# Four-layer hybrid trunk: gate modulation as columns, a third raw weight buffer, an earlier first load, two-pass gate weights

## The chip, the cores and the metric

The kernel runs on 1 core of a Trainium2 chip. The metric is the device time of one execution in microseconds (us); lower is better. The engines are named as the profile does: PE (TensorE's matmuls) and PEld (its weight loads), DVE (VectorE), ACT (ScalarE), POOL (GpSimd), SP (SyncE, which here only issues DMAs). ACT issues some DMAs too.

## The reference

A diffusion trunk of four layers over a latent stream x (512 tokens) and a context stream (256 tokens), both 1024 wide in float32. Layers 0 and 3 are gated linear attention in both directions (GLA), layer 1 is windowed attention, layer 2 a bidirectional RG-LRU. Each is wrapped in normalisation and modulation from a conditioning vector:

```python
for i in range(DEPTH):                                   # 4 layers
    kind, j = i % 3, i // 3
    ctx_out = i < DEPTH - 1
    shift, scale, gate = jnp.split(s_lat @ w_mod[i] + b_mod[i], 3, axis=-1)
    shift_c, scale_c, gate_c = jnp.split(s_ctx @ w_mod[i] + b_mod[i], 3, axis=-1)
    h = rmsnorm(x, g_pre[i]) * (1.0 + scale[:, None, :]) + shift[:, None, :]
    hc = rmsnorm(xc, g_pre[i]) * (1.0 + scale_c) + shift_c
    ...                                                  # y, yc = the layer's mixer of h, hc
    x = x + gate[:, None, :] * rmsnorm(y, g_post[i])
    if ctx_out:
        xc = xc + gate_c * rmsnorm(yc, g_post[i])
# in the GLA mixer, per direction d:
la = log_sigmoid((h @ w_g1[d]) @ w_g2[d] + b_g[d]) / 16  # w_g1 is 1024 x 16, w_g2 is 16 x 512
```

## The kernel before

**Precision.** A float32 operand is held as a rounded high part and the remainder: `Rh` and `Rl` are the normalised, modulated input of both streams (transposed, 8 contraction blocks of 128), and each weight tile becomes `wh` and `wl` (`split`, L265: a cast on ACT, a subtraction on DVE, one in three on POOL). A product is three passes: high by high, high by low, low by high (`ws_part`, L380).

**Weights.** `raw()` (L218) gives 512 KB landing buffers, two in rotation, shared by the weights of the mixers (two to a weight tile, `loadw`, L223), by the modulation's weights (two to a step, `mod_part`, L507) and by some parameters. `fetch` starts one weight ahead, `convert` splits it, `weights` (L358) hands it out. All of these loads are issued in order by SP, which waits there until the buffer is free. In the first normalisation and in two finishes the modulation uses other buffers, `rawp`.

**Modulation.** `mod_part` multiplies 256 columns of `w_mod` by the two conditioning vectors (16 short PE instructions, L524). `mod_ss` (shift and scale) evicts the result, transposes it so that each channel lies on a partition, and adds bias and norm weight there in small DVE operations (L543 to L555). `mod_gate` (gate, four for each layer) loads `g_post` and `b_mod` broadcast over 128 partitions, multiplies (L573 on POOL, L574 on DVE), splits the product (L575, L576) and spreads it over all partitions by four products with a selecting matrix `sel` (L582), which DVE adds to the bias into `gpt` (L583). These steps run inside the mixers, by `background` (L596): a step is begun there and ended at the next call.

**The start.** `first_norm` (L652) loads x and the context, normalises and transposes them, and loads modulation weights in four steps of two parts; the gate weights `w_g1` are fetched ahead of step 1, the first q/k weights ahead of step 3. A hand-written order on PE, ACT and DVE then alternates the modulation products, `modulate` (L697) and the products of the gate weights (`todo[:2]`) and of q and k (`todo[2:]`) over contraction blocks (L734 to L754).

**Gates of GLA.** `load_g1` (L271) puts four copies of `w_g1` into both `wh` and `wl`; the second product (L979) then takes three groups of 32 rows, so that it has the three passes in its own contraction.

**The end of a layer.** `finish` (L758) is the output product over four weight tiles (L796), squares and gates the result (`take`, L801), adds it to the stream (`residual`, L816), normalises (`square`, L819; `scale`, L822) and transposes (`norm`) the next layer's input, two tiles of 128 tokens at a time, in a hand-written order (L884 to L933). `rstd_of` (L611) gives the inverse root in two POOL operations.

**Head 0 of GLA.** `spread` (L1259) deals the matmuls of `values` between the eight steps of `levels`; for the first head of a layer the credit is two thirds of them, and the rest follows.

Elsewhere PE's order comes from a planner that places instructions by program order, priority and its own estimate of when their inputs are ready; each engine runs its list in order.

## Time and profile before

| | us |
|---|---|
| median of three runs (1516.42 to 1520.79) | 1518.22 |
| the profiled execution | 1513.64 |
| its span | 1511.8 |
| PE busy, share of the span | 1442.0 (95%) |
| DVE busy | 1010.5 (67%) |
| ACT busy | 784.2 (52%) |
| POOL busy | 189.4 (13%) |

One execution was profiled; its span runs from the first instruction to the last, and its own time has the launch around it. A busy engine is one with an instruction running; matmuls overlap, so their spacing and not their length is what one more of them costs. "Idle before, released by" names what ended a wait. PEclk is the share of the full clock that PE was granted.

### The profile page before, as it was taken

Reading aid. Unit: us, or ns where it says so; the run is one execution under the profiler, and the core shown is the slowest. Engines: PE = TensorE matmul, PEld = TensorE weight load, DVE = VectorE, ACT = ScalarE, POOL = GpSimd, SP = SyncE. Lnnn points to the kernel's source line nnn. Section 1 sums busy time; section 2 is a strip of 40 time slices with the busy share of each in tenths; the row PEclk is TensorE's granted clock in tenths of the full one; section 3 lists DMA queues with packets and bytes.
Section 4 is the critical chain, followed back from the end, with each engine's and each line's share of the span. In section 5 each row is a group of like instructions: output and inputs, shape, how many; then the busy total and the mean of one; then the engine's idle time right before and its main releaser. Section 6 shows DMA issues by size and latency. Waiting matters only on the chain.

```text
span 1511.8 us, 29077 instructions
## 1 busy us (share of the span) xinstructions
PE 1442.0 (95%) x11691; PEld 1206.4 (80%) x11691; DVE 1010.5 (67%) x1914; ACT 784.2 (52%) x1541; POOL 189.4 (13%) x300
## 2 busy tenths in 40 slices
PE   5988999999999899999999999899999999999998
PEld 3877888888877778878888787788878778889886
DVE  5576657576264389787883568988972667676854
ACT  5535353624252367656662477878842555364441
POOL 2202100112022200010000210000011211101111
PEclk8999999999999999999999999999999999999999
DMA  9441514112574542122216625212252342121232
GB/s 300 145 147 53 169 38 135 57 34 76 203 237 140 174 112 68 31 65 57 57 56 224 217 79 152 82 50 71 67 177 64 103 145 91 46 60 57 60 111 85
DMA packets 153046, 162.35 MB, mean 107 GB/s; under 512 B 12418, under 2 KB 141968, under 8 KB 152912
## 3 DMA queue, kind: packets, MB, share of 16 engines
q1 hardware_dynamic: 147456, 146.56, 31.4%
q10 hardware_dynamic: 5456, 13.94, 2.6%
q8 instruction: 92, 1.51, 0.4%
q14 instruction: 42, 0.34, 0.1%
HBM read 138.44 MB, written 11.53 MB: 99 GB/s over the span
## 4 chain that ended last, share of the span: by engine, by line
PE 54%; DVE 10%; ACT 5%; DMA 4%; issue 2%; SPq 1%; POOL 1%; ACTq 0%; DVEq 0%; POOLq 0%
PE mxt L796 14%; PE pjt L395 9%; PE pjt L385 9%; PE pjt L1034 4%; PE mxt L1532 3%; PE mxt L1516 2%; PE sct L1637 2%; PE mxt L524 1%; PE mxt L1475 1%; PE mxt L1194 1%; DVE wl L269 1%; PE mxt L1458 1%; DMA bb<-in_b_mod_dram 1%; DMA raw<-in_w_mod_dram 1%; PE sct L1062 1%
## 5 line engine op out<-in xcount | busy, mean ns | idle before, releaser
L385 PE MATMUL pjt<-Rh,wh 128*128 128x256 f32 (+1 forms) x592 | 199.0, 337 | 5.3 <-DVE Rh L649 3.3
L385 PE MATMUL pjt<-Rl,wh 128*128 128x256 f32 (+1 forms) x592 | 198.2, 336 | 2.0 <-DVE Rl L650 1.6
L385 PE MATMUL pjt<-Rh,wl 128*128 128x256 f32 (+1 forms) x592 | 197.1, 334 | 0.7 <-DVE wl L269 0.7
L269 DVE TENSOR_TENSOR wl<-raw,wh 128x1024 fp32r<-128x1024 f32 x106 | 129.7, 1237 | 51.2 <-ACT wh L266 50.6
L395 PE MATMUL pjt<-Rh,wl 128*128 128x512 f32 (+1 forms) x448 | 160.3, 358 | 0.0
L395 PE MATMUL pjt<-Rl,wh 128*128 128x512 f32 (+1 forms) x448 | 159.8, 357 | 0.0
L395 PE MATMUL pjt<-Rh,wh 128*128 128x512 f32 (+1 forms) x448 | 159.5, 356 | 0.0
L266 ACT CAST wh<-raw 128x1024 fp32r<-128x1024 f32 x118 | 121.4, 1051 | 71.6 <-PE mxt L796 33.0
L796 PE MATMUL mxt<-wh,Rh 128*128 128x512 f32 x352 | 138.9, 395 | 0.0
L796 PE MATMUL mxt<-wh,Rl 128*128 128x512 f32 x352 | 137.6, 391 | 0.8 <-DVE Rl L769 0.8
L796 PE MATMUL mxt<-wl,Rh 128*128 128x512 f32 x352 | 137.2, 390 | 0.0
L385 PEld LDWEIGHTS pjt<-Rh,wh 128*128 128x128 f32 x592 | 112.5, 191 | 17.0 <-DVE Rh L649 4.4
L385 PEld LDWEIGHTS pjt<-Rl,wh 128*128 128x128 f32 x592 | 112.6, 190 | 14.6 <-DVE Rl L650 3.8
L385 PEld LDWEIGHTS pjt<-Rh,wl 128*128 128x128 f32 x592 | 112.6, 191 | 12.6 <-DVE wl L269 1.2
L1034 PE MATMUL pjt<-wl,Rh 128*128 128x256 f32 x384 | 110.6, 288 | 0.0
L1034 PE MATMUL pjt<-wh,Rh 128*128 128x256 f32 x384 | 109.8, 286 | 0.0
L1034 PE MATMUL pjt<-wh,Rl 128*128 128x256 f32 x384 | 109.5, 285 | 0.0
L1494 ACT ACTIVATE pe<-mxt,mxs 128x256 f32<-128x256 f32 (+2 forms) x128 | 70.7, 556 | 52.6 <-DVE mxs L1486 51.9
L395 PEld LDWEIGHTS pjt<-Rh,wl 128*128 128x128 f32 x448 | 84.6, 189 | 9.8 <-issue 1.9
L395 PEld LDWEIGHTS pjt<-Rh,wh 128*128 128x128 f32 x448 | 84.7, 189 | 9.2 <-issue 1.2
L395 PEld LDWEIGHTS pjt<-Rl,wh 128*128 128x128 f32 x448 | 84.7, 189 | 9.2 <-issue 1.3
L804 DVE TENSOR_TENSOR y<-mxt,gpt 128x512 f32<-128x512 f32 x44 | 30.3, 689 | 73.9 <-ACT y L803 73.8
(295 smaller groups left out, 3480.9 us busy)
## 6 DMA issues: line engine op xcount, KB each, us to landing
rawp<-in_w_mod_dram SPq DMA_DIRECT2D x48, 512.0 KB, 5.8
raw<-in_w_mod_dram SPq DMA_DIRECT2D x48, 512.0 KB, 4.4
raw<-in_a_w_in_dram SPq DMA_DIRECT2D x32, 512.0 KB, 3.5
raw<-in_b_w_in_dram SPq DMA_DIRECT2D x20, 512.0 KB, 4.9
raw<-in_c_w_in_dram SPq DMA_DIRECT2D x20, 512.0 KB, 3.6
xd<-x SPq DMA_DIRECT2D x18, 512.0 KB
raw<-in_a_w_out_dram SPq DMA_DIRECT2D x16, 512.0 KB, 3.5
x<-xd ACTq DMA_DIRECT2D x16, 512.0 KB, 8.9
```

The costliest lines, as they stand in the source:

```text
L266: S.copy(h, x)
L269: e.tensor_tensor(l, x, h.bitcast(F32), op=ALU.subtract)
L385: PE.matmul(ps, w[u][:, k, c0 : c0 + P], R[v][:, k, t0 : t0 + n], start=(k == 0 and u + v == 0), stop=(k == KC - 1 and u == 1),)
L395: PE.matmul(ps, w[u][:, k, c0 : c0 + P], R[x][:, k, t0 : t0 + n], start=(k == 0 and u + x == 0), stop=(k == KC - 1 and u == 1),)
L524: PE.matmul(ps[32 * g : 32 * g + 32, 0:256], sT[:, k, :], r2[k // 4][:, k % 4, :], start=(n < 4), stop=(n >= 4), skip_group_check=True,)
L796: PE.matmul(ps, l[:, tt * P : (tt + 1) * P], r, start=(k == 0 and u + v == 0), stop=(k == kc - 1 and u == 1),)
L804: V.tensor_tensor(y[tt][:, c], ps, gpt[:, 1 if tt >= 4 else 0, c], op=ALU.mult)
L1034: PE.matmul(ps[:, n, :], R[u][:, k, tt * P : (tt + 1) * P], w[x][:, k, :], start=(k == 0 and u + x == 0), stop=(k == KC - 1 and u == 1),)
L1494: S.activation(p[:, o : o + w], u[e][:, :w], AF.Exp, bias=nm, scale=0.125, accum_out=den[:, n : n + 1],)
L1516: PE.transpose(u[e][:, c * P : (c + 1) * P], ps[e][:, m * P : (m + 1) * P], ident)
L1532: PE.matmul(po[64 * e : 64 * e + 64, 0:P], v[:, keys[m], 64 * kv : 64 * kv + 64], pt[:, e, m * P : (m + 1) * P], start=(m == len(keys) - 1 ...
L1637: PE.matmul(ps[:, t0 : t0 + nn], wg[a][:, n, :], x[c][:, p0 : p0 + nn], start=(q == 0), stop=(q == 2),)
```

## The change

The constants and tile `sel` go. `g_post` is loaded once with the other small vectors and transposed into `sm`. `mod_gate` takes the way of `mod_ss` (now `mod_cols`): evict, two transposes, bias and `g_post` on columns; four more transposes, of a column spread over 128 by a step of zero, give the gate on all partitions, and ACT copies it into `gpt`. `raw` has three buffers. `load_g1` makes one tile with three copies of the high part and one of the remainder; its product has two passes (`terms`), and the second product takes all 128 rows. In `first_norm` the gate weights and the first q/k weights are fetched behind step 0, and the products are spread over all steps. In `finish` the last four half products are ordered by tile, and tile 2's residual, square and scale come earlier. The mean's division moves into the square's scale, and epsilon is added on DVE. `spread` has credit for all of the first head's values.

```diff
@@ -130,23 +124,26 @@
-    r1 = sp.tile([64, P], F32, name="r1")
+    r1 = sp.tile([96, P], F32, name="r1")
...
+    nc.scalar.dma_start(r1[64:96, :], I["g_post"].rearrange("l (k p) -> (l k) p", p=P))
...
-    PE.transpose(ps[:, 0:64], r1, ident[:64, :64])
-    PE.transpose(ps[:, 64:160], r3, ident[:96, :96])
-    sm = cp.tile([P, 160], F32, name="sm")
-    V.tensor_copy(sm, ps[:, 0:160])
-    bmT = sm[:, 64:160]
+    PE.transpose(ps[:, 0:96], r1, ident[:96, :96])
+    PE.transpose(ps[:, 96:192], r3, ident[:96, :96])
+    c0 = sp.tile([P, 16], F32, name="c0")
+    V.tensor_copy(c0, ps[:, 0:16])
+    sm = cp.tile([P, 176], F32, name="sm")
+    V.tensor_copy(sm, ps[:, 16:192])
+    bmT = sm[:, 80:176]
...
-    S.activation(cs, sm[:, 0:16], AF.Tanh, scale=0.5)
-    V.scalar_tensor_tensor(cs, cs, 1.0, sm[:, 0:16], op0=ALU.add, op1=ALU.mult)
+    S.activation(cs, c0, AF.Tanh, scale=0.5)
+    V.scalar_tensor_tensor(cs, cs, 1.0, c0, op0=ALU.add, op1=ALU.mult)
@@ -218,7 +215,7 @@
             return raw_pool[0].tile([P, 4, 256], F32, name="rawp", tag="rawp", bufs=10)
-        return wp.tile([P, 4, 256], F32, name="raw", tag="raw")
+        return wp.tile([P, 4, 256], F32, name="raw", tag="raw", bufs=3)
@@ -279,13 +277,12 @@
         def convert():
-            w1h = wp.tile([P, KC, 256], F32R, name="wh", tag="wh")
-            w1l = wp.tile([P, KC, 256], F32R, name="wl", tag="wl")
-            for g in range(4):
-                c = slice(32 * g, 32 * g + 32)
-                S.copy(w1h[:, :, c], rv)
-                V.tensor_tensor(w1l[:, :, c], rv, w1h[:, :, c].bitcast(F32), op=ALU.subtract)
-            return w1h, w1l
+            w1 = wp.tile([P, KC, 256], F32R, name="wh", tag="wh")
+            S.copy(w1[:, :, 0:32], rv)
+            V.tensor_tensor(w1[:, :, 96:128], rv, w1[:, :, 0:32].bitcast(F32), op=ALU.subtract)
+            for g in range(1, 3):
+                S.copy(w1[:, :, 32 * g : 32 * g + 32], w1[:, :, 0:32].bitcast(F32))
+            return (w1,)
@@ -299,7 +296,7 @@
             for d in range(2):
-                for g in range(3):
+                for g in range(4):
                     (nc.sync if d else nc.scalar).dma_start(
@@ -377,14 +374,18 @@
+    def terms(w):
+
+        return ((0, 0), (0, 1), (1, 0)) if len(w) > 1 else ((0, 0), (0, 1))
+
...
         for k in range(KC):
-            for u, v in ((0, 0), (0, 1), (1, 0)):
+            for u, v in terms(w):
                 PE.matmul(
                     ps, w[u][:, k, c0 : c0 + P], R[v][:, k, t0 : t0 + n],
-                    start=(k == 0 and u + v == 0), stop=(k == KC - 1 and u == 1),
+                    start=(k == 0 and u + v == 0), stop=(k == KC - 1 and (u, v) == terms(w)[-1]),
                 )
@@ -541,49 +539,40 @@
-            mt[:, 2 * n : 2 * n + 2, :],
-            pt[:, 0:256].rearrange("p (c g w) -> p c w g", c=2, g=4)[:, :, 0:2, :],
+            mt, pt[:, 0:256].rearrange("p (c g w) -> p c w g", c=2, g=4)[:, :, 0:2, :],
...
-        V.tensor_tensor(
-            mt[:, 2 * n : 2 * n + 2, :], mt[:, 2 * n : 2 * n + 2, :],
-            bt.unsqueeze(2).to_broadcast([P, 2, 2]), op=ALU.add,
-        )
+        V.tensor_tensor(mt, mt, bt.unsqueeze(2).to_broadcast([P, 2, 2]), op=ALU.add)
...
+    def mod_ss(i, n, bank, pool=None, bufs=1):
...
+        if i not in AB:
+            AB[i] = cp.tile([P, 16, 2], F32, name="modT", tag="modT", bufs=2)
+        mt = AB[i][:, 2 * n : 2 * n + 2, :]
+        yield from mod_cols(i, n, mt, bank, pool, bufs)
...
-            g0 = 16 + 8 * i + 2 * (n - 4)
+            g0 = 8 * i + 2 * (n - 4)
...
-                mt[:, 2 * n : 2 * n + 2, :], mt[:, 2 * n : 2 * n + 2, :], 1.0,
-                sm[:, g0 : g0 + 2].unsqueeze(2).to_broadcast([P, 2, 2]), op0=ALU.add, op1=ALU.mult,
+                mt, mt, 1.0, sm[:, g0 : g0 + 2].unsqueeze(2).to_broadcast([P, 2, 2]),
+                op0=ALU.add, op1=ALU.mult,
...
-        gb = wp.tile([P, 256], F32, name="gb", tag="gb", bufs=1)
-        nc.sync.dma_start(
-            gb, I["g_post"][i : i + 1, n * 256 : (n + 1) * 256].to_broadcast([P, 256])
-        )
-        bb = wp.tile([P, 256], F32, name="bb", tag="bb", bufs=1)
-        nc.sync.dma_start(
-            bb, I["b_mod"][i : i + 1, (8 + n) * 256 : (9 + n) * 256].to_broadcast([P, 256])
-        )
-        ps = yield from mod_part(i, 8 + n, bank, pool, bufs)
-        mh = wp.tile([P, 256], F32R, name="mh", tag="mh", bufs=1)
-        ml = (pool or wp).tile([P, 256], F32R, name="ml", tag="mp", bufs=2 if pool else 1)
-        G.tensor_tensor(bb, bb, gb, op=ALU.mult)
-        V.tensor_tensor(gb, ps, gb, op=ALU.mult)
-        S.copy(mh, gb)
-        V.tensor_tensor(ml, gb, mh.bitcast(F32), op=ALU.subtract)
+        mt = cp.tile([P, 2, 2], F32, name="mg", tag="mg", bufs=2)
+        yield from mod_cols(i, 8 + n, mt, bank, pool, bufs)
+        g0 = 48 + 8 * i + 2 * n
+        V.tensor_tensor(mt, mt, sm[:, g0 : g0 + 2].unsqueeze(2).to_broadcast([P, 2, 2]), op=ALU.mult)
...
-        with tc.high_priority(300):
-            for j in range(2):
-                for u, x in enumerate((mh, ml)):
-                    PE.matmul(pt[:, j * 256 : (j + 1) * 256], sel[:, j, :], x, start=(u == 0), stop=(u == 1))
-        V.tensor_tensor(
-            gpt[:, :, n * 256 : (n + 1) * 256], pt.rearrange("p (j n) -> p j n", j=2),
-            bb.unsqueeze(1).to_broadcast([P, 2, 256]), op=ALU.add,
-        )
+        for j in range(2):
+            for c in range(2):
+                PE.transpose(
+                    pt[:, j * 256 + c * P : j * 256 + (c + 1) * P],
+                    mt[:, c, j : j + 1].to_broadcast([P, P]), ident,
+                )
+        S.copy(gpt[:, :, n * 256 : (n + 1) * 256], pt.rearrange("p (j n) -> p j n", j=2))
@@ -608,18 +597,20 @@
-    def rstd_of(pool, ss, n, name):
+    def rstd_of(pool, ss, name, eps=True):
+
...
         r = pool.tile([P, w], F32, name=name, tag=name, bufs=4)
-        G.tensor_scalar(r, ss, 1.0 / n, EPS, op0=ALU.mult, op1=ALU.add)
-        G.tensor_tensor(r, r, nhalf.to_broadcast([P, w]), op=ALU.pow)
+        if eps:
+            V.tensor_scalar(r, ss, EPS, None, op0=ALU.add)
+        G.tensor_tensor(r, r if eps else ss, nhalf.to_broadcast([P, w]), op=ALU.pow)
         return r
...
         ss = pool.tile([P, 1], F32, name="ssx", tag="ssx", bufs=4)
-        S.activation(xn, x, AF.Square, accum_out=ss)
-        return rstd_of(pool, ss, D, "rx")
+        S.activation(xn, x, AF.Square, scale=D ** -0.5, accum_out=ss)
+        return rstd_of(pool, ss, "rx")
@@ -684,13 +675,14 @@
         for n in range(4):
-            if n in (1, 3):
-                fetch()
-                convert()
             for m in (n, n + 4):
...
                 parts.append(f)
+            if n == 0:
+                for _ in range(2):
+                    fetch()
+                    convert()
         if i % 3 == 0:
@@ -724,34 +716,28 @@
                 for k in ks:
-                    for u, v in ((0, 0), (0, 1), (1, 0)):
+                    for u, v in terms(w):
                         PE.matmul(
...
                             start=(k == 0 and u + v == 0 and not (w is wqk and stream == "ctx")),
-                            stop=(k == KC - 1 and u == 1), skip_group_check=True,
+                            stop=(k == KC - 1 and (u, v) == terms(w)[-1]), skip_group_check=True,
                         )
...
                 next(a)
-                if n == 2:
-                    products(todo[:2], range(0, 2))
-                if n == 3:
-                    products(todo[2:], range(0, 3))
                 next(b)
-                if n == 3:
-                    products(todo[:2], range(4, 6))
+                if n:
+                    products(todo[2:], (2 * n - 2,))
                 run(a)
                 run(b)
-                if n == 2:
-                    products(todo[:2], range(2, 4))
-                if n == 3:
-                    products(todo[2:], range(3, 6))
                 modulate(2 * n)
                 modulate(2 * n + 1)
-        products(todo[:2], range(6, 8))
-        products(todo[2:], range(6, 8))
+                if n:
+                    products(todo[2:], (2 * n - 1,))
+                products(todo[:2], (2 * n, 2 * n + 1))
+        products(todo[2:], (KC - 2, KC - 1))
         raw_pool.clear()
@@ -800,15 +786,15 @@
-                S.activation(y[tt][:, c], ps, AF.Square, accum_out=ssq[tt][:, ch : ch + 1])
+                S.activation(y[tt][:, c], ps, AF.Square, scale=D ** -0.5, accum_out=ssq[tt][:, ch : ch + 1])
...
-                s1 = fp.tile([P, 1], F32, name="s1", tag="s1", bufs=4)
-                V.tensor_reduce(s1, ssq[tt], axis=AX.X, op=ALU.add)
-                rs[tt] = rstd_of(fp, s1, D, "ry")
+                s1 = fp.tile([P, 1], F32, name="s1", tag="s1", bufs=2)
+                V.scalar_tensor_tensor(s1, ssq[tt][:, 0:1], EPS, ssq[tt][:, 1:2], op0=ALU.add, op1=ALU.add)
+                rs[tt] = rstd_of(fp, s1, "ry", False)
@@ -899,7 +885,7 @@
                 run(h)
-                h = halves((0, 2), (0, 3), (1, 2), (1, 3))
+                h = halves((0, 2), (1, 2), (0, 3), (1, 3))
                 step((4, 5), 2)
@@ -914,15 +900,15 @@
                 step((0, 1), 0)
+                residual(2)
                 next(h)
                 norm((0, 1), 1)
+                square(2)
                 run(h)
-                residual(2)
                 norm((0, 1), 2)
-                square(2)
+                scale(2)
+                norm((0, 1), 3)
                 residual(3)
-                norm((0, 1), 3)
-                scale(2)
                 square(3)
@@ -953,7 +940,7 @@
             g2 = mp.tile([P, 2, 512], F32R, name="g2")
-            S.copy(g2[:96], g2r[:96])
+            S.copy(g2, g2r)
             G.tensor_tensor(g2[32:64], g2r[32:64], g2[32:64].bitcast(F32), op=ALU.subtract)
@@ -972,12 +959,12 @@
-                    b = sm[:, 48 + 8 * a + 4 * d + h : 49 + 8 * a + 4 * d + h]
+                    b = sm[:, 32 + 8 * a + 4 * d + h : 33 + 8 * a + 4 * d + h]
...
-                            ps[:, t0 : t0 + n], g2[:96, d, h * P : (h + 1) * P], t1[:96, t0 : t0 + n],
+                            ps[:, t0 : t0 + n], g2[:, d, h * P : (h + 1) * P], t1[:, t0 : t0 + n],
@@ -1304,8 +1291,7 @@
                 nz = len(STREAM) * T if ctx_out else len(STREAM) * TL
-                nz = nz if prev else 0
-                spread(lv, side, len(LEVELS), 24 * (nz + 4 * GDV) / 2.4)
+                spread(lv, side, len(LEVELS), 24 * (nz + 4 * GDV if prev else 6 * GDV) / 2.4)
                 run(side)
```

## Rows read from the trace of the kernel before

**Rows 1.** The page, engines: busy us, share of the span, instructions.
```profile
PE 1442.0 (95%) x11691; PEld 1206.4 (80%) x11691; DVE 1010.5 (67%) x1914; ACT 784.2 (52%) x1541; POOL 189.4 (13%) x300
```

**Rows 2.** Stretches: length, busy us (instructions) by engine, PEclk, DMA share, GB/s.
```profile
0.00:62.40 62.40, 46.19 (x314) 33.16 (x315) 32.83 (x70) 30.97 (x55) 18.18 (x30) 0.92 0.77 235
...
62.40:130.00 67.60, 59.30 (x777) 50.27 (x775) 47.77 (x72) 36.17 (x53) 9.43 (x13) 0.97 0.41 125
...
868.40:960.00 91.60, 84.20 (x535) 68.32 (x534) 70.10 (x102) 68.08 (x92) 8.40 (x32) 0.97 0.35 110
```

**Rows 3.** Waits of PE: waiter, releaser, us in total, times, longest us.
```profile
PE mxt L524 <- DMA raw<-in_w_mod_dram: 8.3, 9, 1.5
...
PE sct L1637 <- ACT gt L1643: 1.9, 1, 1.9
...
PE mxt L582 <- ACT mh L575: 1.3, 3, 0.6
```

**Rows 4.** Timeline of the start: start, us, engine, line, operation, count, idle before.
```profile
24.38 2.50 ACT L703 ACTIVATE Rh<-OG,modT 128x256 fp32r<-128x256 f32 x4 [1.37 <-DVE modT L555]
...
48.03 1.07 PE L524 MATMUL mxt<-rawp,sT 128*32 128x256 f32 x16
...
56.85 0.28 PE L728 MATMUL sct<-Rh,wh 128*128 128x256 f32 x1
...
58.95 0.28 PE L728 MATMUL sct<-Rh,wh 128*128 128x256 f32 x1
...
62.41 0.28 PE L385 MATMUL pjt<-Rh,wh 128*128 128x256 f32 x1
```

**Rows 5.** SP's queue at the start, and the page's issues with median us to landing.
```profile
33.88 3.92 SPq L511 DMA_DIRECT2D rawp<-in_w_mod_dram  x4
...
rawp<-in_w_mod_dram SPq DMA_DIRECT2D x48, 512.0 KB, 5.8
```

**Rows 6.** Timeline of PE: transposes of two blocks, and one gate's spreading products.
```profile
51.24 0.38 PE L542 MATMUL pjt<-ident,mp 128*128 128x128 f32 x2
...
51.46 0.38 PE L542 MATMUL mxt<-ident,mp 128*128 128x128 f32 x2
...
77.01 0.39 PE L582 MATMUL mxt<-mh,sel 128*128 128x256 f32 x1
...
77.58 0.28 PE L1034 MATMUL pjt<-wh,Rh 128*128 128x256 f32 x1
```

**Rows 7.** By line: instructions, ns min/median/max, first and last start, forms.
```profile
L574 DVE TENSOR_TENSOR gb<-mxt,gb x16: 391/425/426, 71.4 to 1258.7; 128x256 f32<-128x256 f32 x16
...
L583 DVE TENSOR_TENSOR gpt<-mxt,bb x16: 676/691/693, 77.9 to 1459.6; 128x512 f32<-128x512 f32 x16
...
L543 DVE TENSOR_REDUCE modT<-mxt x28: 161/167/176, 23.8 to 882.4; 128x4 f32<-128x16 f32 x28
```

**Rows 8.** Timeline of layer 2: DVE, SP's queue and PE at one stall.
```profile
947.39 0.68 DVE L269 TENSOR_TENSOR wgl<-raw,wgh 128x512 fp32r<-128x512 f32 x1
...
948.09 0.38 SPq L229 DMA_DIRECT2D raw<-in_c_w_in_dram  x1
...
953.89 0.39 PE L385 MATMUL pjt<-Rh,wh 128*128 128x256 f32 x1 [1.96 <-ACT wh L266]
```

**Rows 9.** Stretches at the lower clock: length, PE busy (instructions), PEclk, DMA.
```profile
26.00:36.00 10.00, 6.80 (x43) 0.50 1.12 328
...
954.00:961.00 7.00, 5.08 (x16) 0.53 0.09 26
```

**Rows 10.** Timeline of PE: transposes of the first inputs.
```profile
12.10 0.85 PE L680 MATMUL mxt<-ident,xp 128*128 128x128 f32 x3
...
16.13 0.60 PE L680 MATMUL pjt<-ident,xp 128*128 128x128 f32 x4
```

**Rows 11.** Timeline of layer 0's end, DVE.
```profile
451.63 1.28 DVE L816 SCALAR_TENSOR_TENSOR x<-y,ry,x 128x1024 f32<-128x1024 f32 x1
...
453.88 3.41 DVE L816 SCALAR_TENSOR_TENSOR x<-y,ry,x 128x1024 f32<-128x1024 f32 x1
```

17 lines of the change are left out of this document (4 added, 13 removed).

## The prediction

> **What bounds the kernel now.** I read the page's engine line first, then the span cut into stretches, then what PE waited for, and only then the timelines. TensorE is busy 95% of the span, 1442.0 of 1511.8 us, and VectorE 67% [rows 1]. So an edit pays in two ways only: it takes matmuls away, or it closes one of PE's holes. The holes hold 1511.8 - 1442.0 = 69.8 us. They are not spread evenly. The first 62.4 us have 62.4 - 46.2 = 16.2 us of them, the first head of layer 0 another 67.6 - 59.3 = 8.3, the beginning of layer 2 another 91.6 - 84.2 = 7.4 [rows 2]. Where the change leaves PE's work alone and PE is full, nothing can come of it. By releaser the largest hole of all is a modulation product waiting for its own weights, 8.3 us in 9 times [rows 3].
>
> The sum is made against the profiled execution, 1513.64 us with 1511.8 of span. The median of the three runs is 1518.22, which is 4.58 us above it; I carry the difference in us over to the median.
>
> **Startup: the loading order, the products behind each modulation step, the two-pass gate weights.** Today PE runs without a hole from the last modulation product at 48.03 to 62.41 [rows 4], so from 48.03 on the start is bound by PE and not by loads. Two contraction blocks of the gate weights' product take 58.95 - 56.85 = 2.10 us, two blocks of the k and q products 62.41 - 58.95 = 3.46 [rows 4], that is 1.05 and 1.73 each. With two passes in place of three a gate block costs 0.70; over eight blocks that removes 8 x 0.35 = 2.8 us. The new order leaves, from the last modulation product on (1.07): one k/q block (1.73), two pairs of transposes (0.44 at the spacing of [rows 6]), a second block (1.73), two gate blocks (1.40) and two k/q blocks (3.46), in all 9.8 us. The last two blocks must wait for their activations, which took 2.50 us in the first step [rows 4]; 1.73 of it is covered, and VectorE's subtraction follows, so I add 1.5. That gives 11.3 against 62.41 - 48.03 = 14.4, a gain of 3.1 with the product where it was.
>
> The product can also come sooner. Its four loads leave SP's queue from 33.88 on, over 3.92 us, so by 37.8, and such a load takes 5.8 us to land [rows 5]: the data are there near 43.6, but the product stands in PE's order behind three k/q blocks. In the new order only one block is ahead of it. Moving the first q/k weights (1 MB in four issues) ahead on SP's queue delays the loads of steps two and three that it is moved past, not the last ones, as the bytes ahead of them are the same. I take 2.4 of the 4.4 us, since the earlier blocks must first be worked off. Startup in all: **-5.5**, with bounds of -2 (the loads of the middle steps land late and PE idles there instead) and -8.
>
> The same edit in layer 3 again removes 2.8 us of matmuls, and three of four weight subtractions. But half of those matmuls stand where PE follows VectorE's normalisation of the next tiles: **-1.2**, bounds 0 and -2.8.
>
> **Third raw buffer.** Layer 2 shows what two cost. SP issues the second half of a gate projection's weights at 948.09, 0.02 us after a subtraction frees the buffer (947.39 + 0.68); the casts follow and PE has stood 1.96 us when it restarts at 953.89 [rows 8], then 1.9 more for a gate activation queued behind the casts [rows 3]. The granted clock then reads 0.53 of full over 954 to 961 [rows 9], so 5.08 us of work lose about 2.4. A third buffer lets that half go with the first. All of it would be 6.3 us; **-4.5**, since PE may find another wait in the same place; bounds 0 and -6.3.
>
> The 8.3 us of waits for modulation weights [rows 3] have the same origin: each step needs two buffers, and its second load waits for a product or a subtraction. Three buffers free one load of the two. **-4**, bounds 0 (the other load still lands last) and -8.3. A queue effect belongs here: dropping the two broadcast loads of each gate removes 32 issues from SP's queue, ahead of weights. I count nothing for it, since the weights are held by buffers; it is cover for the 4.
>
> **The gates as columns.** On PE, four spreading products (77.58 - 77.01 = 0.57 us) go; two transposes (51.46 - 51.24 = 0.22) and four more (0.44 at that spacing) come [rows 6]. That is +0.09 with no break between; each change of operand adds some 0.1, as the products' first step shows in its longer 0.39. I take +0.25 for each of 16 gates, **+4**. The trace has no operation that loads one column spread over 128 as weights; the nearest row, the transposes, says that it costs the same, so 1.5 is one end; the other is 13.6, if each gate also waits 0.6 us for its columns (PE's three waits of this kind averaged 0.43 [rows 3]). On VectorE, 0.43 + 0.43 (the second subtraction, of the same size) + 0.69 go and three small operations of at most 0.17 come [rows 7]: -1.0 for each. That reaches the end only where VectorE limits PE, in layer 0's first head and at the beginning of layer 2: **-1.5**, bounds 0 and -6. ScalarE gains one copy of 128 x 512; it is busy 52% [rows 1] and I cost it at nothing. If that cover is missing, it is no more than VectorE's 0.69 for this size, 11 us for 16. GpSimd loses its multiplication, which nothing waits for but VectorE's product.
>
> [...]
>
> **Finish and the smaller edits.** Tile 2 of each finish is completed one product earlier and its residual moved ahead; tile 3's residual goes behind the last two normalisation groups. Both sit in VectorE's queue, where one residual takes 1.28 us, but the last one of layer 0 took 3.41 [rows 11]. What tile 2 gains tile 3 gives back, as the transposes need both; what can be won is the stretch of 2.1 us, once. The epsilon moves from GpSimd to VectorE, where it waits in order for ScalarE's square. Behind it stand the last tile's gating and a normalisation, which wait for PE anyway; without that cover it is a hold of about 1.3 us, by the activations of 768 columns (2.50 for two [rows 4]), in each of three finishes. **-1**, bounds -3.4 and +4. First-head values dealt over all steps: PE has spare time between the level products, but the levels follow VectorE and ScalarE; **-0.5**, bounds -3 and +2.
>
> **The sum.** -5.5 - 1.2 - 4.5 - 4 + 4 - 1.5 - 1 - 0.5 = -14.2. The profiled execution would take 1499.4, the median 1518.22 - 14.2 = **1504.0**.
>
> **Rivals.** *Loads no sooner* (0.18): the third buffer only moves the wait to the next load in SP's order, and the start idles in its middle steps. For it: the start is full of loads (DMA share 0.77 [rows 2]). Against it: 948.09 is released by a buffer. Startup then gives 2.75, the stall 0, the modulation waits 1: -2.75 - 1.2 - 1 + 4 - 1.5 - 1 - 0.5 = -4.0, so 1514.3, no difference that shows.
>
> *The gate's second hand-over* (0.11), the case on the slower side. The four last transposes wait for three small VectorE operations in the same step, where today a whole step lies between. If these stand behind a long VectorE operation, PE, in order, waits too. Everything else brings -18.2; sixteen gates cost 16 x (0.25 + w). It decides from w = 0.89 on. At w = 1.5, two of VectorE's middle-sized operations, it is 28.0 - 18.2 = +9.8: 1528.0. For it: VectorE is busy 70.1 of 91.6 us where layer 2's gates lie [rows 2]. Against: today's three such waits sum to 1.3.
>
> [...]
>
> *The start keeps its clock and the loads are all early* (0.10): today 10 us from 26 on run at 0.50, with 6.80 us of work [rows 9], which costs 3.4. With k/q blocks to fill that stretch it may go; with the rest of layer 3's passes (1.6) and all modulation waits (4.3): -23.5, so 1494.7.
>
> **Chances and range.** My forecast has 0.58, with a range of its own of 1497 to 1511. Leaving out the slower case and half of the lowest one, 1494 to 1517 should hold 8 in 10. About 0.3%, 4.6 us, is what a measurement of this kernel can tell from no change; the three runs spread by as much. Faster: 0.58 + 0.10 and some of the first rival, 0.72. Slower: 0.12. Within: 0.16.
>
> **What would show it.** Right: the first product of the ctx q block, now at 62.41, begins near 57; no PE hole of 2 us before a cast in layer 2; PE's waits on modulation weights below 4.5 us; two passes over the gate weights. Wrong: spreading transposes that wait on columns for more than 0.9 us on average; a hole in the start between steps two and three as long as what the end gains; a stretch at the lower clock at each layer's gates.

## The result, and the profile after

The changed kernel takes 1539.88 us (median of 1531.39 to 1543.81) where the kernel before takes 1518.65 beside it: a ratio of **1.0132, 95% interval 1.0094 to 1.0170**, some 20 us slower. The forecast was 1504.0, range 1494 to 1517. The profiled execution's span is 1538.1 us, against 1511.8 before: 26.3 us more.

The first view is the page's engine line of the changed kernel: busy time, share of the span, instructions.

```profile
PE 1450.3 (94%) x11683; PEld 1205.4 (78%) x11683; DVE 997.7 (65%) x1952; ACT 789.6 (51%) x1555; POOL 153.0 (10%) x218
```

Beside [rows 1], VectorE and GpSimd do less, as was meant. PE issues eight instructions fewer and is busy 8.3 us longer, and its holes grew from 69.8 to 1538.1 - 1450.3 = 87.8 us. So two thirds of the loss are holes. The busy time needs an explanation of its own, and it has one below: matmuls at a granted clock of 0.51.

The second view is PE's waits in the changed kernel: waiter, releaser, us in total, times, longest.

```profile
PE mxt L571 <- DVE mg L566: 11.2, 3, 6.0
PE mxt L525 <- DMA raw<-in_w_mod_dram: 8.4, 7, 3.0
...
PE mxt L629 <- DVE y L809: 6.2, 4, 3.3
PE mxt L1194 <- DVE on L1187: 6.1, 11, 0.9
PE sct L720 <- POOL Rl L700: 6.0, 7, 1.4
...
PE sct L720 <- ACT Rh L695: 3.5, 2, 2.1
```

Five of these waits are new or have grown: the gates' spreading transposes (L571) on the third small VectorE operation of their columns (L566), the finish's transposes (L629) on a scaled row (L809), the head transposes of the GLA layers (L1194) on the scaled head (L1187), and the start's products (L720) on each of the two halves of their activations. In the kernel before, the gates' products waited 1.3 us for ScalarE's high half [rows 3] and 0.6 once for VectorE's remainder, the head transposes also 1.3 in 4 times, the finish's 1.8 in 2. The wait that led there, for modulation weights, is 8.4 us now and was 8.3.

If one follows the same PE instruction through both traces, the distance between them says where the time goes: +5.5 us when the start's last product is through (the next product begins at 67.95, before at 62.41), +9.4 when layer 0's output products begin, back to +6 early in layer 1 (the modulation products there no longer wait), and then two jumps: 8.1 us at the end of layer 1's attention and 8.6 us at the end of layer 3. This is the first of them, the timeline of VectorE and PE in the changed kernel (start, us, engine, line, operation, count, idle before):

```profile
795.90 1.31 PE L1518 MATMUL mxt<-pt,v 128*64 128x128 f32 x20
...
797.14 0.44 PE L540 MATMUL mxt<-ident,mp 128*128 128x128 f32 x2
...
800.23 0.16 DVE L541 TENSOR_REDUCE mg<-mxt 128x4 f32<-128x16 f32 x1
800.31 1.21 DVE L266 TENSOR_TENSOR wl<-raw,wh 128x1024 fp32r<-128x1024 f32 x1
...
801.44 0.75 DVE L755 TENSOR_TENSOR Rl<-OGb,Rh 128x256 fp32r<-128x256 f32 x2
...
802.11 0.15 DVE L546 TENSOR_TENSOR mg<-mg,sm 128x4 f32<-128x4 f32 x1
802.19 1.22 DVE L266 TENSOR_TENSOR wl<-raw,wh 128x1024 fp32r<-128x1024 f32 x1
...
803.32 0.15 DVE L566 TENSOR_TENSOR mg<-mg,sm 128x4 f32<-128x4 f32 x1
...
803.62 1.09 PE L571 MATMUL mxt<-ident,mg 128*128 128x128 f32 x4 [6.04 <-DVE mg L566]
...
804.36 0.78 PE L782 MATMUL mxt<-wh,Rh 128*128 128x512 f32 x1
```

PE transposes the last gate of the layer at 797.14 and next in its order stand the four spreading transposes. They need three VectorE operations of 0.15 us each. The first runs only at 800.23, behind operations on the layer's activations, and after each of the first two VectorE takes a weight subtraction of 1.2 us first (and between them two more of the layer's activations). So PE stands for 6.04 us, with the output products queued behind. The same place in the kernel before:

```profile
789.32 1.31 PE L1532 MATMUL mxt<-pt,v 128*64 128x128 f32 x20
...
790.56 0.39 PE L582 MATMUL mxt<-mh,sel 128*128 128x256 f32 x1
...
791.14 0.39 PE L796 MATMUL mxt<-wh,Rh 128*128 128x512 f32 x1
```

From the attention's last product to the first output product it is 1.82 us there and 8.46 in the changed kernel. The wait has an after-effect, in the stretches of the changed kernel (length; busy us and instructions of PE, its weight loads, VectorE, ScalarE and GpSimd; granted clock; DMA share and GB/s):

```profile
797.00:804.30 7.30, 1.26 (x10) 0.91 (x7) 6.47 (x16) 3.61 (x7) 0.95 (x1) 0.75 0.71 228
804.30:807.50 3.20, 3.20 (x10) 2.55 (x10) 0.00 (x0) 0.59 (x1) 0.00 (x0) 0.51 0.99 346
...
1478.70:1484.70 6.00, 1.12 (x5) 0.71 (x5) 5.46 (x12) 3.59 (x7) 0.00 (x0) 0.88 0.30 96
1484.70:1490.20 5.50, 5.50 (x15) 4.33 (x15) 0.35 (x2) 0.59 (x1) 0.00 (x0) 0.51 1.01 344
1490.20:1496.00 5.80, 5.80 (x27) 4.75 (x26) 0.00 (x0) 0.00 (x0) 0.00 (x0) 1.00 0.30 120
```

PE is busy 1.26 of 7.30 us, and when it starts again the granted clock reads 0.51 for 3.2 us; at the end of layer 3 it waits 4.88 us and then runs 5.5 us at 0.51. An output product is 0.78 us long at 804.36 and 0.39 in the kernel before at 791.14, and the longer time counts as busy. So an estimate from these rows is 3.2 x 0.49 + 5.5 x 0.49 = 1.6 + 2.7 = 4.3 us, about half of the 8.3 by which busy PE grew.

The start, PE's timeline in the changed kernel:

```profile
31.09 0.58 PE L720 MATMUL sct<-Rl,wh 128*128 128x256 f32 x1 [1.43 <-POOL Rl L700]
...
33.31 1.94 PE L525 MATMUL pjt<-rawp,sT 128*32 128x256 f32 x16
...
56.58 1.04 PE L525 MATMUL mxt<-rawp,sT 128*32 128x256 f32 x16
...
67.71 0.40 PE L720 MATMUL sct<-Rh,wl 128*128 128x512 f32 x1
```

The last modulation product begins at 56.58, where before it began at 48.03 [rows 4], and the start's last product at 67.71, where before PE had gone on to the next weights at 62.41 [rows 4]. The forecast had it 5.5 us earlier.

### The profile page after: what moved, and what is told of

Read it like the earlier page. It is cut to its first block, busy times and chain, and to the rows that moved or that the text cites. A ratio compares the mean times of both kernels' runs of the same rounds, so it can differ in the third digit from the quotient of the medians.

```text
span 1538.1 us, 28936 instructions
## 1 busy us (share of the span) xinstructions
PE 1450.3 (94%) x11683; PEld 1205.4 (78%) x11683; DVE 997.7 (65%) x1952; ACT 789.6 (51%) x1555; POOL 153.0 (10%) x218
## 5 line engine op out<-in xcount | busy, mean ns | idle before, releaser
L386 PE MATMUL pjt<-Rl,wh 128*128 128x256 f32 (+1 forms) x592 | 198.2, 337 | 5.0 <-DVE Rl L641 4.9
L386 PE MATMUL pjt<-Rh,wh 128*128 128x256 f32 (+1 forms) x592 | 199.9, 340 | 2.6 <-DVE Rh L640 1.6
L386 PE MATMUL pjt<-Rh,wl 128*128 128x256 f32 (+1 forms) x568 | 190.3, 336 | 0.0
L386 PEld LDWEIGHTS pjt<-Rl,wh 128*128 128x128 f32 x592 | 111.9, 189 | 19.4 <-DVE Rl L641 7.3
L386 PEld LDWEIGHTS pjt<-Rh,wh 128*128 128x128 f32 x592 | 112.2, 190 | 16.6 <-DVE Rh L640 3.5
L386 PEld LDWEIGHTS pjt<-Rh,wl 128*128 128x128 f32 x568 | 107.0, 189 | 12.7
L396 PEld LDWEIGHTS pjt<-Rh,wl 128*128 128x128 f32 x448 | 84.4, 188 | 10.2 <-issue 1.9
L782 PEld LDWEIGHTS mxt<-wh,Rh 128*128 128x128 f32 x352 | 67.2, 191 | 16.4 <-issue 0.8
```

The costliest lines, as they stand in the source:

```text
L386: PE.matmul(ps, w[u][:, k, c0 : c0 + P], R[v][:, k, t0 : t0 + n], start=(k == 0 and u + v == 0), stop=(k == KC - 1 and (u, v) == terms(w)[ ...
L396: PE.matmul(ps, w[u][:, k, c0 : c0 + P], R[x][:, k, t0 : t0 + n], start=(k == 0 and u + x == 0), stop=(k == KC - 1 and u == 1),)
L782: PE.matmul(ps, l[:, tt * P : (tt + 1) * P], r, start=(k == 0 and u + v == 0), stop=(k == kc - 1 and u == 1),)
```

## The experiments

Theory A, formed from these views: the loss lies in four separate places (the gate's hand-over, the start, epsilon on VectorE, the finish's order), and the rest of the change brings about what was forecast. The rival: the parts that stay (columns, transposes, a third buffer and its loads) are themselves dear, and the waits only show it. Each of the first four kernels is the changed kernel with one part undone; the later ones start from the kernel in which all four are undone. All ratios are to the kernel before on the same chip; 0.001 is 1.52 us.

### A step between a gate's columns and its spreading

```
                 f = f(*a, mxt)
                 next(f)
                 next(f, None)
+                if gate:
+                    next(f)
                 if open_bg:
                     run(open_bg.pop())
```

> The changed kernel, with one edit: as soon as a gate's modulation product is opened, its two transposes and the three small VectorE operations that make the columns are issued too, so that only the spreading transposes are left for the next background step (a whole step lies between, as in the kernel before). Theory A, the hand-over: in the changed kernel the spreading transposes waited 6.04 us at 797 and 4.88 us at 1479 behind VectorE's queue at the ends of layers 1 and 3, and the distance to the kernel before grew there by 8.1 and 8.6 us, lower clock included. Both waits go, and the time is 1539.9 - 16 = 1524 us (1519 to 1529). [...]

Measured: 1523.75 us, ratio 1.0040 (1.0023 to 1.0057), 0.0092 or 14.0 us less than the changed kernel. Theory A. In its trace no spreading transpose waits for its columns at the end of layer 1 (L785 is the output product here):

```profile
797.42 1.31 PE L1521 MATMUL mxt<-pt,v 128*64 128x128 f32 x20
...
798.66 0.65 PE L571 MATMUL mxt<-ident,mg 128*128 128x128 f32 x4
...
799.07 0.48 PE L785 MATMUL mxt<-wh,Rh 128*128 128x512 f32 x1
```

It is 1.65 us from product to product, against 1.82 before the change, and the granted clock reads 1.00 there and behind it, from 798.0 to 806.0. The waits of 6.04 and 4.88 us and the 4.3 us estimated for the clock of 0.51 behind them make 15.2; the runs give 14.0. The instructions are the same in number and kind, so the reading that the columns themselves are dear falls.

### The start's old order

```
         for n in range(4):
+            if n in (1, 3):
+                fetch()
+                convert()
             for m in (n, n + 4):
...
-            if n == 0:
-                for _ in range(2):
-                    fetch()
-                    convert()
...
                 next(a)
+                if n == 2:
+                    products(todo[:2], range(0, 2))
+                if n == 3:
+                    products(todo[2:], range(0, 3))
                 next(b)
```

(and so on: the products stand again where the kernel before has them)

> The changed kernel with the first normalisation's order of before: the first two weights fetched at steps one and three, the products a step behind their activations; the gate weights keep two passes. Theory A, the rounds: in the changed kernel each step's products follow that step's own activations, PE waits for them in every step (POOL's Rl 6.0 us in 7 waits, ScalarE's Rh 3.5 in 2) and the next step's modulation product stands behind them; the start was 5 us longer than before by the time the first ctx q product was through. With the old order that goes, and the two passes' 2.8 us come on top: 1539.9 - 5 - 2 = 1533 us (1530 to 1536). Rival B, the loads: the start is longer because the small first loads (one more of them) and the weights land later; then the order of the products is worth nothing, 1538 to 1542.

Measured: 1530.98 us, ratio 1.0098 (1.0078 to 1.0118): 5.2 us less. The start's last product begins at 62.24 instead of 67.71. In the trace the start is 5.5 us shorter; by the time alone the loss is not clear, as this interval overlaps that of the changed kernel. Beside the four edits, below, it is. Whether the products' order (A) or the loads (B) cost it is open here, as both were undone. Two later kernels take them apart.

### Epsilon back on GpSimd

```
         if eps:
-            V.tensor_scalar(r, ss, EPS, None, op0=ALU.add)
+            G.tensor_scalar(r, ss, EPS, None, op0=ALU.add)
```

> The changed kernel with the addition of epsilon back on GpSimd for the head normalisations of the GLA layers and the row normalisations (one more GpSimd operation, one VectorE operation fewer in each). Theory A: on VectorE the addition waits in order behind the gating product of 0.69 us, and the transposes after it waited 6.1 us in 11 times against 1.3 in 4 before; the layers with heads lost about 2.5 and 1.5 us. So 1539.9 - 4 = 1536 us (1533 to 1538). Rival B: GpSimd's operation is no faster there (1.05 to 1.18 us beside a busy VectorE in the kernel before), and it is the same, 1538 to 1542.

Measured: 1527.68 us, ratio 1.0079 (1.0055 to 1.0102): 8.0 us less, twice what A had, though the interval overlaps that of the changed kernel a little. The waits of the head transposes fall from 6.1 us to

```profile
PE mxt L1194 <- DVE on L1187: 1.7, 5, 0.6
```

which is 4.4 us of the 8.0. Another part shows in the start, ahead of any head: its last product begins at 64.59 instead of 67.71, 3.1 us sooner. The last two kernels take heads and rows apart.

### The finish's old order

```
-                h = halves((0, 2), (1, 2), (0, 3), (1, 3))
+                h = halves((0, 2), (0, 3), (1, 2), (1, 3))
```

(and the residuals, squares and scales of tiles 2 and 3 where the kernel before has them)

> The changed kernel with the order of before in the finish: output halves (0,2), (0,3), (1,2), (1,3), the residual of tile 2 after the second normalisation group, that of tile 3 before the last group. Theory A: the transposes that wait for tile 3's scaled rows stood 6.2 us in 4 times in the changed kernel, 3.47 in one hole, against 1.8 in 2 before; moving back gives 2 to 4 us: 1539.9 - 3 = 1537 us (1535 to 1539). Rival B: what tile 3 lost tile 2 had gained (the hole of 2.12 us in the first finish of the kernel before comes back), no change: 1538.5 to 1542.

Measured: 1534.06 us, ratio 1.0119 (1.0098 to 1.0141): 2.0 us less, within the interval of the changed kernel, so the time alone doesn't tell. The wait does: 6.2 us on the scaled row become

```profile
PE mxt L629 <- DVE y L809: 1.8, 2, 1.0
```

as before the change, while the next products' waits on their activations shift (L386 on Rh from 1.6 to 4.9, on Rl from 4.9 to 2.2). Some of what one tile lost another had gained, as rival B said; 2 us net is the best estimate, and it isn't shown to differ from nothing.

### All four mended

> The changed kernel with the four edits measured so far together (a step between a gate's columns and its spreading, the start's old order, epsilon on GpSimd, the finish's old order). What stays of the change: columns and transposes for the gates, the third raw buffer, the two-pass gate weights, mean in the square's scale, the dealt values. Theory A: the four losses lie at different places, and what stays is the gain that was forecast, so they nearly add: 1537.5 - 14.0 - 5.2 - 8.0 - 2.0 = 1508 us against 1517.4 before; epsilon's gain lies partly in the start, which the old order alters anyway, so 1506 to 1513. Rival B: what one edit gives back is a wait that another then takes (the same engines), and the kernel ends where the kernel before does, 1515 to 1519.

Measured: **1506.10 us, ratio 0.9927 (0.9912 to 0.9941)**, faster than both kernels. The four differences add up to 0.0192 and would give 0.9940; so they lie in different places and hardly overlap, and the parts of the change that stay are worth 11 us together. Theory A. PE's engine line, of the fastest of the six executions (1503.18 us):

```profile
PE 1434.4 (96%) x11683; PEld 1195.6 (80%) x11683; DVE 993.5 (66%) x1908; ACT 788.9 (53%) x1555; POOL 172.3 (11%) x262
```

PE has the same 11683 instructions as in the changed kernel, is busy 15.9 us less (the mean granted clock is 0.992 here, 0.983 there) and idle 1501.4 - 1434.4 = 67.0 us instead of 87.8.

### The start: loads or order?

Two kernels beside the one with four edits: one with the changed kernel's early weights and the products a step behind their activations, one with the changed kernel's start whole.

```
                 next(a)
                 next(b)
                 if n:
+                    products(todo[:2], (2 * n - 2, 2 * n - 1))
                     products(todo[2:], (2 * n - 2,))
...
-                products(todo[:2], (2 * n, 2 * n + 1))
+        products(todo[:2], (KC - 2, KC - 1))
```

> As the one with four edits, but the start keeps the change's early weights and takes another cure for its order: the products of each step follow the next step's modulation product, so that each stands one step behind its own activations. Theory A: the change's start lost by the order of its products alone; with the early weights and a lag it is at least as good as the old order, 0 to 5 us faster than the four edits together, near 1506 us. Rival B: the early weights push the modulation weights of the middle steps back (1 MB ahead of them on SP's queue), and PE waits for those: 2 to 4 us slower than the four edits together, near 1512.

> As the one with four edits, but with the start of the changed kernel (early weights, each step's products behind that step's own activations): its distance to the one with four edits (1506.1) is the whole price of the new start, and its distance to the lagged start with the same loads (1510.5) the price of the products' order alone. By the ends of the start's products (61.22 us with the old order, 64.43 lagged with early weights, 67.71 in the changed kernel) half is the loads, half the order: 1506.1 + 6.5 = 1513 us (1511 to 1515). Rival: the loads are all of it and the order nothing, near 1510.5.

Measured: 1510.48 us, 0.9953 (0.9937 to 0.9969), with the lag; 1512.66 us, 0.9968 (0.9951 to 0.9984), with the changed kernel's start. So the new start costs 0.0041 or 6.2 us in all. With the lag 3.9 of them remain, and the last 2.3, the order's share, are less than the intervals tell apart: whether the order costs anything by itself is not shown. What the cure of the order does is seen in PE's waits from 20 to 68 us, first with the changed start, then with the lag:

```profile
PE sct L723 <- POOL Rl L703: 6.0, 7, 1.8
PE sct L723 <- ACT Rh L698: 1.6, 1, 1.6
```

```profile
PE pjt L525 <- DMA rawp<-in_w_mod_dram: 7.7, 1, 7.7
PE mxt L525 <- DMA rawp<-in_w_mod_dram: 1.2, 1, 1.2
PE sct L723 <- POOL Rl L703: 0.4, 1, 0.4
```

7.6 us of waits on activations go, and 8.9 us of waits for modulation weights stand in their place: with the lag, the second step's product waits for its weights until 30.52, with the changed start it begins at 31.63, held by activations, and in the kernel with four edits at 24.8. The start's last product begins at 64.43 with the lag, 63.66 without and 61.22 with the old order. So 1 MB of other weights ahead of the second step's weights is enough to make that step late, and each later step with it; curing the order of the products gains nothing for the start while the loads stand as they do. My half-and-half split of the expectation falls for the start's own length; on the whole time it is not refuted.

A third kernel takes the old places of the loads and the lag:

> As the one with four edits, with the first weights fetched at steps one and three (as before), and the products a step behind their activations in each step, not gathered in the last two. Theory A: with the modulation weights first on the queue no step is late, and the products fill the 2.9 us in which the one with four edits waits at 38.9 for the last step's weights: 1 to 3 us faster, near 1504. Rival B: the gate and k/q weights land only near 39 us, so the products of steps one and two wait for them and the modulation product behind them is late: 1 to 4 us slower.

Measured: 1512.78 us, 0.9969 (0.9951 to 0.9986), 6.4 us slower than the one with four edits: rival B. PE's waits from 20 to 68 us show it:

```profile
PE sct L722 <- ACT wh L263: 4.7, 1, 4.7
PE pjt L525 <- DMA rawp<-in_w_mod_dram: 2.2, 1, 2.2
```

The products of the second step wait 4.7 us for their own weights, and the modulation product stands behind them. Old loads and gathered products belong together.

### The third buffer

```
-        return wp.tile([P, 4, 256], F32, name="raw", tag="raw", bufs=3)
+        return wp.tile([P, 4, 256], F32, name="raw", tag="raw", bufs=2)
```

> As the one with four edits, but with two raw buffers. Theory A: the third buffer is worth what the distance to the kernel before lost at the second layer's modulation products (4 us between 490 and 530 us) and in layer 2 (2 us near 950): 6 us slower than the four edits together, near 1515 us, with waits for modulation weights up by 4 us or more and the 2-us hole before a cast in layer 2 back. Rival B: those gains come from the 32 broadcast loads that no longer stand in SP's queue; then two buffers do as well, within 2 us.

Measured: 1512.08 us, 0.9962 (0.9950 to 0.9975), 0.0035 or 5.3 us slower than with three. Theory A. PE's waits, with two buffers:

```profile
PE mxt L525 <- DMA raw<-in_w_mod_dram: 13.0, 13, 2.1
...
PE sct L1631 <- ACT gt L1637: 2.8, 2, 2.2
```

and with three:

```profile
PE mxt L525 <- DMA raw<-in_w_mod_dram: 8.4, 7, 2.4
```

4.6 us of modulation waits and 2.6 us on layer 2's gate activation (2.8 against 0.2) come back with two buffers. The hole before a cast in layer 2 did not come back, so that part of A's sign was wrong: the wait stands at the activation instead.

### The old gates

The kernel with two buffers, and the gate modulation of before (broadcast loads, selector products, no columns).

> As the one with two raw buffers, but with the gate modulation of before too (broadcast loads, products with the selector, no columns). Theory A: once a step lies between, columns and products cost PE about the same, and VectorE's 1 us for each gate is hidden: within 3 us of the one with two raw buffers. Rival B, the columns themselves are dear (96 transposes, a second hand-over): 4 to 8 us faster than that. Rival C, the broadcast loads cost (32 loads ahead of weights on SP's queue): 3 to 6 us slower.

Measured: 1521.44 us, 1.0029 (1.0018 to 1.0040): 0.0067 or 10 us slower than with columns. So beside these edits columns, once a step lies between, are worth 10 us, which none of the three expectations had in size; rival C has the sign. In the profiled executions it is 5.9 us (spans of 1518.2 and 1512.3), and the views show a sum of small things. Two stretches, with the old gates, then with columns:

```profile
940.00:965.00 25.00, 20.46 (x99) 15.31 (x98) 21.88 (x30) 19.59 (x23) 1.47 (x2) 0.86 0.36 115
...
500.00:510.00 10.00, 7.76 (x46) 5.73 (x45) 1.65 (x2) 1.19 (x3) 0.00 (x0) 0.83 0.57 183
```

```profile
940.00:965.00 25.00, 22.17 (x119) 18.32 (x120) 22.21 (x35) 22.77 (x27) 0.00 (x0) 0.93 0.27 85
...
500.00:510.00 10.00, 8.61 (x64) 6.60 (x60) 1.00 (x6) 2.30 (x5) 0.00 (x0) 1.00 0.52 157
```

and the second of them in the kernel before, which has the old gates too:

```profile
500.00:510.00 10.00, 8.60 (x56) 6.23 (x53) 1.93 (x4) 0.99 (x2) 0.73 (x1) 1.00 0.55 172
```

With the old gates PE gets fewer instructions through in each (99 against 119, 46 against 64), at a lower granted clock (0.86 and 0.83 against 0.93 and 1.00), and a cast's wait of 2.0 us (L392 on ACT wh) is there again in layer 2. Whether the broadcast loads or VectorE's three wider operations are the cause wasn't tried apart; that stays open.

The 10 us are no gain on the kernel before, though. The kernel with the old gates keeps the two passes, the dealt values, the mean in the square's scale, epsilon in the row sums of the finish and one more small first load, and with these it is 0.0029 or 4.4 us slower than the kernel before, its interval clear of 1. If one follows PE through both traces, it falls behind by 3.4 us between 460 and 480 us, 1.7 between 910 and 940 and 3.6 near 1270, and near these places it falls behind the columns too. From 500 to 510 us the clock stays at 1.00 in the kernel before, with the same gates. So the old gates alone do not explain what is lost there: the other parts, or how the gates fall in with them, have a share, and which of them wasn't tried. Against the kernel before, columns and those parts with two buffers give 0.0038 or 5.8 us (0.9962).

### The two passes and the dealt values

> As the one with four edits, but the gate weights again in three passes (four copies with their own low parts). Theory A: the third pass is worth 2.8 us of matmuls in the start, which is bound by TensorE from 51 us on, and 1.2 in layer 3: 1506.1 + 4 = 1510 us. Rival B: the start is bound by its loads and the passes lie in their shade: within 1.5 us of 1506.

> As the one with four edits, but the first head's values products again all left for the end of the level products (the dealing counts nothing for a head without one before it). Theory A: the levels follow VectorE and ScalarE, and products dealt between them fill PE's idle time, 2 to 4 us in the two first heads: 1506.1 + 3 = 1509 us. Rival B: the products are needed anyway and fill the next wait instead: within 1 us of 1506, as the prediction had it (-0.5).

Measured: 1508.25 us, 0.9937 (0.9918 to 0.9957), with three passes; 1507.95 us, 0.9937 (0.9914 to 0.9959), with the old deal. Both intervals overlap that of the kernel with four edits: each is worth 1.5 us at best estimate and neither can be told from nothing by the time. For the passes the trace adds that the start's last product begins at 62.99 instead of 61.22, 1.8 us of the 2.8 forecast.

### Which epsilon?

```
-            G.tensor_scalar(r, ss, EPS, None, op0=ALU.add)
+            (V if name == "ro" else G).tensor_scalar(r, ss, EPS, None, op0=ALU.add)
```

> As the one with four edits, but epsilon on VectorE for the head normalisations of the GLA layers alone (20 small operations). The edit of epsilon gave 8.0 us where the waits of the heads' transposes (6.1 us in 11 against 1.7 in 5) explain 4.4. Theory A, the heads: those waits come back, 1506.1 + 4 = 1510 us (1508 to 1513). Rival B: the heads' waits are filled by other products, and the gain lay in the row normalisations: within 1.5 us of 1506.

> As the one with four edits, but epsilon on VectorE for the row normalisations alone (24 operations, in the start and in the finishes). Theory A, the rows: the rest of the 8.0 us lies here, most of it in the start, where six tiles follow one another, and where the trace with the edit was 3 us shorter by 50 us: 1506.1 + 4 = 1510 us (1508 to 1512). Rival B: the start of that trace was shorter because the casts of the first weights came elsewhere in ScalarE's order, which the old order of the start settles anyway: within 1.5 us of 1506.

Measured: heads 1514.29 us, 0.9981 (0.9968 to 0.9993), 8.2 us slower than the kernel with four edits; rows 1506.91 us, 0.9945 (0.9932 to 0.9959), 2.7 us by the ratio, with overlapping intervals. So beside the old start the heads carry it: 20 operations of 0.16 us. Beside the changed start, whose last product came 3.1 us sooner with epsilon on GpSimd, the row normalisations may have a part that these two kernels do not show. The trace with the heads on VectorE, then the one without, at the same head:

```profile
214.74 0.69 DVE L1192 TENSOR_TENSOR on<-mxt,gh 128x512 f32<-128x512 f32 x1 [0.37 <-ACT on L1191]
...
215.35 0.16 DVE L608 TENSOR_SCALAR ro<-sso 128x2 f32<-128x2 f32 x1
215.59 0.69 POOL L609 TENSOR_TENSOR ro<-ro,nhalf 128x2 f32<-128x2 f32 x1 [24.73 <-DVE ro L608]
...
216.31 0.62 DVE L1195 TENSOR_SCALAR on<-on,ro 128x256 f32<-128x256 f32 x2 [0.80 <-POOL ro L609]
```

```profile
209.92 0.69 DVE L1192 TENSOR_TENSOR on<-mxt,gh 128x512 f32<-128x512 f32 x1 [0.38 <-ACT on L1191]
209.97 0.22 POOL L608 TENSOR_SCALAR ro<-sso 128x2 f32<-128x2 f32 x1 [23.95 <-ACT on L1191]
...
210.27 0.71 POOL L609 TENSOR_TENSOR ro<-ro,nhalf 128x2 f32<-128x2 f32 x1
...
211.02 0.62 DVE L1195 TENSOR_SCALAR on<-on,ro 128x256 f32<-128x256 f32 x2 [0.41 <-POOL ro L609]
```

On VectorE the addition stands behind the product of 0.69 us that starts when the squares are done, and the head is scaled 1.57 us after that product's start. On GpSimd the addition runs beside the product, and it is 1.10 us. If each of the 20 pairs of head tiles loses 0.47 us like this one, that is 9.4 us in all, of which PE's waits show 4.4. That the rest reaches PE through what stands behind on VectorE, which itself idles 0.80 us for the power in place of 0.41, is argued and not shown. The addition takes 0.16 us on VectorE and 0.22 on GpSimd, and the time is 8.2 us shorter on GpSimd, so the operation's own length does not decide.

## Why the prediction was wrong

**What bounds the kernel** held: TensorE is full (busy 94 to 96% of the span in the kernel before, the changed one and the one with four edits), and what moved the time were its holes and the granted clock of 0.51 behind two of them.

**The gates.** The rival of the second hand-over was described as it came (small VectorE operations in the same step, PE in order behind them), with a chance of 0.11. Two steps of it failed. The evidence against it, that the waits of before summed to 1.3 us [rows 3], came from a kernel in which a whole step lay between, so it said nothing of one without; it also left out the 0.6 us on VectorE's remainder. And the price was a mean over 16 gates with a threshold of 0.89 us. The waits came to 11.2 / 16 = 0.70 us, below it, and the kernel was slower all the same. For one thing the threshold took the rest to bring -18.2, which the start and epsilon did not let it. For another the waits sat in two places, at the last gate of layers 1 and 3, which no later background step picks up and which the finish runs to its end together with its weight subtractions. The second and the third small operation each queued behind one of these, the first behind the layer's activations; I had priced two operations of VectorE, once. The granted clock of 0.51 behind each of the two was not in the price. The place could have been read from the code and from VectorE's queue where the finish begins.

The other half, the columns' own cost, was mis-sized with the wrong sign: +4 on PE and -1.5 by VectorE, a loss of 2.5. The runs show 10 us in the columns' favour with two buffers once the hand-over is mended, against a kernel that is itself 4.4 us slower than the kernel before. A clock that falls with the columns' transposes had 0.03 of the chances, and no run shows one. With those transposes the mean granted clock is 0.988, with the selector products 0.985 (0.988 to 0.991 and 0.984 to 0.988 over all executions). In the changed kernel the clock was down before the gates' transposes came: it reads 0.50 from 801.0 to 803.6 and from 1483.5 to 1484.0, with no PE instruction in either stretch. With the same transposes and no wait it reads 1.00 (798.0 to 806.0, with a step between).

**The start.** The step that failed is the sentence that the moved weights delay the loads of the middle steps, not the last ones, so that the end gains. The second step's product began at 30 to 33 us instead of 24.2 to 24.8, and as each step's activations, products and transposes follow one another on PE, the lateness of the second step is that of the last. I had also charged the wait for a step's own activations to the last step alone (1.5 us); in the changed kernel it comes in each of the four. My sign for it, a hole between the middle steps as long as what the end gains, was the right one to look for: there PE waits on activations, 9.5 us from 20 to 68 us. Not all of the late end was this: 3.1 us of it went with epsilon's return to GpSimd alone. The term of -5.5 had 2.8 of the passes in it, so -2.7 stands against the +6.2 that the new start costs beside the old one with two passes.

**The third buffer.** -4.5 and -4 were forecast, 8.5 in all; taking it away costs 5.3 to 6.0 us (by ratio, by medians), with 4.6 us of modulation waits of it. The mechanism was right, the stall's half too large.

**Epsilon.** I costed it in the three finishes (a hold of 1.3 us each, bounds -3.4 and +4 together with the finish's order) and not where it is used most, in the 20 head normalisations. There it is worth 8.2 us beside the old start. That step skipped a use of the function it had to cost. The rows of the start and of the finishes' normalisations come to 2.7 us beside the old start, which can't be told from nothing; beside the changed start their share is open.

**Finish order, two passes, dealt values.** -1 for the finish's order came out as +2 at best estimate, within its bounds and not told from nothing by the time, and against the reading that the two tiles give and take; -2.8 and -1.2 for the passes as about -1.5; -0.5 for the values as about -1.5, neither clear of noise.

Summed up: the change without its four losses is worth -11.1 us (0.9927). What the forecast had for the parts that stay is -2.8 - 1.2 - 4.5 - 4 + 4 - 1.5 - 0.5 = -10.5, and that this is so near is luck: the columns, forecast as a loss of 2.5, differ by 10 us from the old gates, the third buffer by 5.3 where 8.5 were forecast, passes and values by some 1.5 each, and the kernel without columns and third buffer is 4.4 us slower than the kernel before, a loss that no term had and whose cause is open. The losses, 14.0 + 5.2 + 8.0 + 2.0 = 29.2 us, were in the text as a rival, a bound or a sign, except for the heads, which are missing. The range of 1494 to 1517 had no room for several of them at once.

## What to carry to other kernels

When a step is split into more hand-overs, look at where the last instance of it is drained: there is no step left to lie between, and its small operations queue behind whatever the next stage has already issued (here PE waited 6.0 and 4.9 us for them). An operation's place in a busy engine's queue can cost more than its length: 0.16 us twenty times cost 8.2 us here. A load moved ahead on a busy queue can make every chain late that begins with the loads behind it (here the second step's product began at 30 to 33 us in place of 24.2 to 24.8); cost it at the first of them, not at the last. And a part's worth holds for the kernel it was measured in: the columns' 10 us were measured against a kernel that stood behind the kernel before.

## What the runs showed of the hardware

After waits of 6.04 and 4.88 us the granted clock read 0.51 for the next 3.2 and 5.5 us of full work, so these two holes cost some 40% more than they showed: 10.9 us of holes came with 4.3 us lost in slow work, by the estimate from those rows. Without the first hole the clock read 1.00 in the same place (798.0 to 806.0, in the kernel with a step between). Without the second, output products there started 0.23 us apart (1472.43 and 1472.66); behind the hole it was 0.43 (1486.20 and 1486.63).

On GpSimd the addition on two columns took 0.22 us beside VectorE's 0.16. A weight subtraction took 2.46 us on GpSimd and 1.22 on VectorE (medians of the changed kernel), so the two engines lie further apart there; it differs from the addition in size and in operation, and which of these decides wasn't tried.
